# A chunked RWKV scan on one core: planned lengths, no fill matmuls, one direction with its halves swapped, and outputs stored by ScalarE's queue

## The chip, the cores and the metric

The kernel runs on one core of one Trainium2 chip. A core has five engines that run their own instruction streams in order and meet at semaphores: TensorE (PE; its weight loads are shown apart as PEld), VectorE (DVE), ScalarE (ACT), GpSimd (POOL) and SyncE (SP), which issues most of the transfers. The metric is the device time of one execution in microseconds; lower is better. Before the change it is 3036.94 us, the median of three runs (3034.74 to 3039.24).

## The reference

Two layers of a generator work on 1024 latent tokens and 256 context tokens of width 1024, in float32. The first layer mixes tokens with a bidirectional RWKV-7 scan, the second with a grouped 2-D Fourier transform; an MLP of hidden width 4096 follows each. The part that the change touches is the scan, which is run for 16 heads of width 64 in both directions:

```python
def step(s, inp):
    w_t, k_t, v_t, a_t, b_t = inp[:5]
    sa = jnp.einsum('bhvk,bhk->bhv', s, a_t)
    s = s * w_t[:, :, None, :] + sa[..., None] * b_t[:, :, None, :] + v_t[..., None] * k_t[:, :, None, :]
    y = jnp.einsum('bhvk,bhk->bhv', s, inp[5]) if with_out else None
    return s, y

for d in range(N_DIRS):
    rev = d == 1
    yc, s_ctx = _wkv_scan(st_c.get('r'), vh_c, *st_c['dirs'][d], s0, rev)
    yl, _ = _wkv_scan(st_l['r'], vh_l, *st_l['dirs'][d], s_ctx, rev)
```

The context gives the first 256 positions of each direction (no output is read from them), and the latents start from the state that it leaves.

## The kernel before, in words

**Stages.** The kernel projects the streams (up to about 634 us of the span), scans (634 to about 1250 us), and then does the readout, the two MLPs and the Fourier layer.

**Projections.** `factor` (L781) makes, for one direction and 128 channels, the four scaled factors of the scan in chunks of 64 positions, in the tiles `bk_` and `ar`, and stores them in DRAM (`s_bk`, `s_ar`). Four element-wise products on DVE or POOL (recorded at L460) write them.

**The scan.** It runs in 20 steps of 64 positions, 4 for the context and 16 for the latents; a step does both directions d for all 16 heads. In `scan_step`: the *scores* (L951) multiply the b and k factors with the a and r factors; ACT (L960, L964) and DVE (L967, L972) evict them with masks. The scores of b with a are a strictly triangular 64x64 matrix M per head and direction, and the recurrence inside a chunk needs the inverse of (1 - M). `scan_invert` makes it: DVE inverts 16x16 blocks (L1074 to L1104), PE joins them to 32x32 blocks with the matmul groups *H* (L1141) and *T* (L1154), and the 32x32 block off the diagonal of the 64x64 inverse comes from two more groups, *V* (L1173) and *G* (L1184): V = M's block times one diagonal inverse, copied out of PSUM (L427, tile `vt`), G = V times the other diagonal inverse, copied into the inverse's tile `tt` (L427 again). *turn* (L1130) transposes the b and k factors. After that comes the part that goes from step to step: *x* (L1008), a copy, *u* (L1017, which reads `tt`), copies into `sv`, *s* (L1031, the new state), an addition (L1037) and a scaling (L993) on DVE, and two copies of the state into the next step's `sv`. For latents the outputs are *r* (L1047) and *y* (L1053) into one bank, a copy by ACT into the tile `y` (L1059), and a store of 64x1024 values to `s_y`.

In H and T the four groups of 32 partitions each have their own rows and columns of the PE array. In V and G before the change the forward and backward direction both keep the off-diagonal block in the same place: V reads partition groups 0 and 2 only and writes 1 and 3, and G the other way round. So each is 32 matmuls of 32x32 on two groups, and the copies are two of 32x512 each.

**Order and queues.** The whole program is a list of operations with planned lengths. `Plan.emit` (L165) simulates the engines with these lengths and writes each engine's instructions in the order in which the simulation starts them. It also models PE's clock, which it takes to be halved when PE's weighted activity (`load`) of the previous interval was low. Where an operation opens a fresh PSUM bank and PE is planned to be idle before it, it writes *fill* matmuls into that bank (L230 to L233; the fill itself is L1843, identity times identity, and its result is overwritten). On the chip nothing looks at planned times any more: each engine takes its instructions in the written order and waits where a semaphore is not there yet.

SP issues the scan's loads (L916: `s_bk`, `s_ar`, `s_v`), the stores to `s_y` (also L916), and loads of modulation weights (L892, 128x512 pieces of `k_mwt`), which DVE multiplies and sums in between (L893). A store waits at SP for ACT's copy L1059, and what stands behind it at SP waits too. The ring of `y` tiles has two places, that of `bk` four.

```python
if e == "pe" and blank:
    fills = max(0, int((start - since - self.SLACK) / self.FILL))
    for _ in range(fills):
        since = self.clock(since, self.FILL, 1.0)
    start = max(start, since)
```

Of the kernel before, what the change touches and what calls it, by code (L numbers as in the profile page):

```python
# [18 lines left out]
P = 128  # L19
# [3 lines left out]
CTX = 256  # L23
# [57 lines left out]
class Plan:  # L81
# [10 lines left out]
    def __init__(self, nc, banks, engines, hold=None):  # L92
        self.nc, self.engines, self.hold = nc, engines, hold or (lambda d: 0.7)
        self.psum = Store(banks)
        self.ops, self.last, self.seen, self.uses = [], {}, {}, {}
        self.step, self.rank = None, 0.0
        self.dear, self.weigh, self.follows = {}, {}, {}
# [11 lines left out]
    def add(self, eng, dur, fn, r=(), w=(), bank=None, after=(), load=1.0, lag=None, hold=None):  # L109
        bases = [k[0] if isinstance(k[0], tuple) else k for k in (*r, *w) if not isinstance(k, Slab)]  # L110
        gates = []
        for k in bases:
# [3 lines left out]
            if g is not None:  # L116
# [4 lines left out]
                  hold=hold, dear=self.dear, weigh=self.weigh)  # L121
# [43 lines left out]
    def emit(self):  # L165
# [26 lines left out]
        while done < len(ops):  # L192
# [86 lines left out]
    ("bk", (8, P), *_row(4, "X0", 0, 1024)), ("mab", (2, 16, 32), *_row(3, "X1", 0, 1024)), ("tr", (16, 32), ("X1", 3072)), ("vt", (16, 32), ("X1", 3584)),  # L279
# [51 lines left out]
class Kernel:  # L331
# [449 lines left out]
    def factor(self, kt, low, d, c, k, k_k, kk, kkk, rr):  # L781
# [57 lines left out]
    def scan(self):  # L839
# [10 lines left out]
        for j, tt in enumerate(R["tt"]):  # L850
            for g in (1, 3):
                plan.add("pool", 0.6, lambda tt=tt, g=g: nc.gpsimd.memset(tt[32 * g : 32 * g + 32, :, 0:32], 0.0), (), [(("tt", j), g)])
# [4 lines left out]
        for i in range(NCH):  # L857
            self.plan.step = i
            self.scan_step(i)
# [47 lines left out]
    def scan_step(self, i):  # L907
# [3 lines left out]
        RZ = [[slice(hh * 64 + 32 * z, hh * 64 + 32 * z + 32) for hh in range(2)] for z in range(2)]  # L911
# [24 lines left out]
        for d in range(2):  # L936
# [5 lines left out]
            for h4 in range(2):  # L942
# [11 lines left out]
                plan.add("pe", 0.95, mms, [kb, (kL, "a", 0), (kL, "a", 1)],  # L954
                         [*BB, *[k for hh in range(2) for k in ((kM, d, hh, h4, 0), (kM, d, hh, h4, 1), (kL, "k", hh, h4), (k2, hh, h4))]])
                for hh, B in enumerate(BB):
# [4 lines left out]
                        mab[RZ[0][hh], :, ys].rearrange("p w q t -> p q w t"),  # L961
                        B.tile[RZ[0][hh]].rearrange("p (q w t) -> p q w t", q=4, w=4)[:, :, 0:2], AF.Copy, scale=-0.5),
                        [B], [(kM, d, hh, h4, 0)], B)
                    plan.add("act", 0.28, lambda bv=bv, hh=hh, ys=ys, d=d: nc.scalar.activation(  # L964
                        mab[RZ[1][hh], 0, ys], bv()[RZ[1][hh], :, 32:C], AF.Copy, scale=-0.5),
# [32 lines left out]
        for d in range(2):  # L998
# [11 lines left out]
            self.at = plan.add("pe", 0.95, x_mm, lall + vall, [B], B, load=0.95)  # L1010
# [9 lines left out]
            plan.add("pe", 0.95, u_mm, [kx, *kT], [U], U, load=0.5)  # L1020
# [3 lines left out]
            if i < NCH - 1:  # L1024
# [10 lines left out]
                plan.add("pe", 1.1, s_mm, vall + [(kt_, 0), (kt_, 1)], [B, kt0], B, load=0.78)  # L1035
# [3 lines left out]
            if lat:  # L1039
# [10 lines left out]
                def y_mm(B=Y, l2=l2, sv=sv):  # L1050
# [5 lines left out]
                plan.add("pe", 0.95, r_mm, vall + [E["ks"], (kL, "a", 0), (kL, "a", 1)], [Y], Y, load=0.5)  # L1056
                plan.add("pe", 1.05, y_mm, vall + [(k2, hh, h4) for hh in range(2) for h4 in range(2)], [Y], Y, load=1.0)
                y, ky = slot("y")
                plan.add("act", 0.58, lambda B=Y, y=y: nc.scalar.copy(y, B.tile), [Y], [ky], Y)  # L1059
                dma(self.s_y[d, E["lo"] - CTX : E["lo"] - CTX + C].rearrange("t (h c) -> h t c", h=2), y, 256, [ky],  # L1060
                    [("sy", d, (E["lo"] - CTX) // C)])

    def scan_invert(self, mab, kM, S):
# [60 lines left out]
        def turned(d):  # L1124
# [7 lines left out]
            plan.add("pe", 0.85, turn, [S[d]["kb"]], [*TB[d]], load=0.5)  # L1132
# [10 lines left out]
        for w in range(2):  # L1143
            plan.add("pe", 0.7, lambda w=w: h_mm(w), [kxt, *ms], [(H, w)], load=0.15)
# [11 lines left out]
        for w in range(2):  # L1156
            plan.add("pe", 0.75, lambda w=w: t_mm(w), [khp, kxd], [(T, w)], load=0.3)
# [11 lines left out]

        def v_mm():  # L1170
            for y in range(16):
                for g in (0, 2):
                    nc.tensor.matmul(V.tile[Q[g + 1], y * 32 : y * 32 + 32], mab[Q[g], 1, y, :], tr[Q[g], y, :], start=True, stop=True)  # L1173

        plan.add("pe", 0.75, v_mm, [ktr, *offs], [V], V, load=0.15)
        vt, kvt = slot("vt")
        for g in (1, 3):
            plan.flex({"act": 0.58, "dve": 0.69}, lambda e, g=g: self.copy_on(e, vt[Q[g]].rearrange("p y t -> p (y t)"), V.tile[Q[g]]),
                      [V], [(kvt, g)], V)

        def g_mm():
            for y in range(16):
                for g in (1, 3):
                    nc.tensor.matmul(G.tile[Q[g - 1], y * 32 : y * 32 + 32], vt[Q[g], y, :], tt[Q[g], y, 32:64], start=True, stop=True)  # L1184

        plan.add("pe", 0.75, g_mm, [(kvt, 1), (kvt, 3), (kT, 1), (kT, 3)], [G], G, load=0.15)
# [3 lines left out]
        return tt, [(kT, g) for g in range(4)] + [(kT, g, "o") for g in (0, 2)]  # L1190
# [40 lines left out]
    def late(self):  # L1231
        plan = self.plan
        plan.dear, plan.weigh = REST_DEAR, REST_WEIGH
# [635 lines left out]
def host_consts():  # L1869
# [8 lines left out]
    for hh in range(2):  # L1878
        b, k = slice(hh * 64, hh * 64 + 64), slice((1 - hh) * 64, (1 - hh) * 64 + 64)
        mask[b, 0, hh], mask[k, 0, hh] = np.concatenate([-0.5 * strict, -0.5 * incl], 1), np.concatenate([strict, incl], 1)  # L1880
        mask[b, 1, hh] = np.concatenate([-0.5 * strict, -0.5 * incl[:, ::-1]], 1)
        mask[k, 1, hh] = np.concatenate([strict[::-1], incl[::-1, ::-1]], 1)
# [72 lines left out]
```

## Time and profile before

| | |
|---|---|
| median of three runs | 3036.94 us (3034.74 to 3039.24) |
| the profiled execution: its own time, its span | 3052.24 us, 3050.2 us |
| mean granted TensorE clock of that execution | 0.947 of full speed |
| PE busy in the span | 2858.6 us (94%) |
| DVE, ACT, POOL busy in the span | 1880.4, 1014.3, 487.8 us |
| the scan stage, 634 to 1250 us | 616 us, PE busy 510.5 us, DVE 422.4, ACT 349.2 |

All times inside the execution are microseconds from the start of the span. A group of instructions is told as: line, engine, operation, output tile <- input tiles, shapes, count | busy us, mean ns of one | idle time of the engine ahead of them and what ended it. A float32 matmul appears as two matmul instructions in the trace, so 32 matmuls of the program are a group of x64.

### The profile page before, as it was taken

How to read it: one execution, taken by the hardware profiler on the slowest of the kernel's cores; microseconds unless marked ns; L12 is line 12 of the kernel's file. 1: busy time of each engine (PE TensorE's matmuls, PEld its weight loads, DVE VectorE, ACT ScalarE, POOL GpSimd, SP SyncE). 2: the span in 40 equal slices, each digit the busy share in tenths (PEclk: the TensorE clock that was granted, in tenths of full speed). 3: DMA queues.
4: the chain of work that ended last, by engine and by line, in shares of the span. 5: the costliest groups of instructions: out<-in, count | busy, mean ns of one | idle time of the engine just before them, and what ended most of it. 6: DMA issues, size and time to landing. Idle time of an engine off the chain costs nothing.

```text
span 3050.2 us, 63412 instructions
## 1 busy us (share of the span) xinstructions
PE 2858.6 (94%) x26844; PEld 2225.1 (73%) x26844; DVE 1880.4 (62%) x3363; ACT 1014.3 (33%) x1974; POOL 487.8 (16%) x415
## 2 busy tenths in 40 slices
PE   9999989988887888799999999999899999999998
PEld 5443446467777777688788888887798788888887
DVE  5398695546667666787655665454876554454455
ACT  4263454345555555333212111112322111111121
POOL 2063453300000000111110111010421110111110
PEclk9999999968789897799999999999899999999999
DMA  9266475623345443643222322211121111111111
GB/s 280 83 180 185 129 195 172 181 83 101 113 125 154 124 124 120 205 132 97 90 86 90 111 90 90 63 62 34 47 76 42 56 49 49 42 56 49 35 45 56
DMA packets 297293, 312.90 MB, mean 103 GB/s; under 512 B 81025, under 2 KB 212225, under 8 KB 297009
## 3 DMA queue, kind: packets, MB, share of 16 engines
q1 hardware_dynamic: 295648, 304.01, 33.3%
q8 instruction: 210, 3.44, 0.5%
q0 software_dynamic: 1360, 4.84, 0.5%
q14 instruction: 75, 0.61, 0.1%
HBM read 246.38 MB, written 62.39 MB: 101 GB/s over the span
## 4 chain that ended last, share of the span: by engine, by line
PE 78%; DVE 10%; DMA 4%; issue 4%; ACT 3%; SPq 1%; POOL 1%; DVEq 0%; ACTq 0%; POOLq 0%
PE ps L368 17%; PE ps L370 17%; PE ps L369 17%; PE ps L624 6%; PE ps L621 4%; PE ps L951 3%; PE ps L1843 2%; DVE bU L460 1%; PE ps L1008 1%; PE ps L1031 1%; PE ps L1017 1%; PE ps L1154 1%; PE ps L578 1%; PE ps L1053 1%; PE ps L1141 1%
## 5 line engine op out<-in xcount | busy, mean ns | idle before, releaser
L368 PE MATMUL ps<-rU,rU 128*128 128x512 f32 (+3 forms) x2632 | 980.1, 372 | 16.8 <-DVE rX L1538 8.0
L370 PE MATMUL ps<-rU,rU 128*128 128x512 f32 (+3 forms) x2632 | 976.1, 371 | 6.2 <-DVE rU L1268 3.5
L369 PE MATMUL ps<-rU,rU 128*128 128x512 f32 (+3 forms) x2632 | 975.9, 371 | 0.1
L368 PEld LDWEIGHTS ps<-rU,rU 128*128 128x128 f32 x2632 | 501.5, 191 | 111.9 <-DVE rX L1538 8.9
L370 PEld LDWEIGHTS ps<-rU,rU 128*128 128x128 f32 x2632 | 501.5, 191 | 97.8 <-DVE rU L1268 4.8
L369 PEld LDWEIGHTS ps<-rU,rU 128*128 128x128 f32 x2632 | 501.9, 191 | 90.3 <-DVE rU L1352 0.4
L1538 DVE SCALAR_TENSOR_TENSOR rX<-ps,mods,rX 128x512 f32<-128x512 f32 (+1 forms) x528 | 375.6, 729 | 123.8 <-PE ps L370 121.7
L1517 ACT ACTIVATE rS<-ps 128x512 f32<-128x512 f32 x122 | 73.0, 598 | 681.5 <-PE ps L370 680.8
L1268 POOL TENSOR_TENSOR rU<-rW,rU 128x512 fp32r<-128x512 f32 x73 | 118.0, 1621 | 1001.6 <-PE ps L370 518.3
L624 PE MATMUL ps<-bU,bU 128*128 128x512 f32 (+1 forms) x544 | 235.1, 568 | 2.6 <-ACT bS L427 1.9
L427 ACT CAST rU<-rW 128x512 fp32r<-128x512 f32 x161 | 97.2, 617 | 349.0 <-PE ps L370 260.9
L1268 DVE TENSOR_TENSOR rU<-rW,rU 128x512 fp32r<-128x512 f32 x201 | 173.3, 881 | 25.4 <-ACT rU L427 25.3
L427 DVE CAST rU<-rS 128x512 fp32r<-128x512 f32 (+1 forms) x97 | 45.0, 469 | 232.8 <-ACT rS L1520 205.4
L427 DVE CAST rU<-rW 128x512 fp32r<-128x512 f32 x115 | 55.1, 491 | 212.6 <-PE ps L369 210.3
L624 PEld LDWEIGHTS ps<-bU,bU 128*128 128x128 f32 x544 | 99.5, 191 | 108.2 <-issue 96.3
L621 PE MATMUL ps<-bU,bU 128*128 128x512 f32 x304 | 140.9, 604 | 0.0
L951 PE MATMUL ps<-sU,sX 64*128 64x128 f32 (+1 forms) x1280 | 119.3, 338 | 17.5 <-DVE sU L967 5.9
L951 PEld LDWEIGHTS ps<-sU,sX 64*128 64x128 f32 x1280 | 105.7, 241 | 24.7 <-issue 6.6
L427 ACT COPY sU<-ps 32x512 f32<-32x512 f32 (+1 forms) x167 | 96.2, 577 | 79.6 <-PE ps L1154 27.6
L967 DVE TENSOR_TENSOR sU<-ps,sW 64x256 f32<-64x256 f32 x160 | 67.5, 422 | 70.7 <-ACT sX L960 39.1
L1268 POOL TENSOR_TENSOR rU<-rS,rU 128x512 fp32r<-128x512 f32 x41 | 64.1, 1566 | 289.8 <-ACT rU L427 154.8
L1843 PE MATMUL ps<-ident 128*128 128x128 f32 x664 | 98.9, 308 | 2.8 <-DMA ident<-in_k_ident_dram 2.6
(275 smaller groups left out, 3740.8 us busy)
## 6 DMA issues: line engine op xcount, KB each, us to landing
rW<-in_mlp_w_dram SPq DMA_DIRECT2D x256, 256.0 KB
rW<-in_k_mwt_dram SPq DMA_DIRECT2D x96, 256.0 KB
sX<-s_bk SPq DMA_DIRECT2D x40, 512.0 KB
s_ar<-bU SPq DMA_DIRECT2D x32, 512.0 KB
sU<-s_ar SPq DMA_DIRECT2D x64, 256.0 KB
sW<-in_k_mwt_dram SPq DMA_DIRECT2D x64, 256.0 KB
bU<-in_rk_wk_dram SPq DMA_DIRECT2D x48, 256.0 KB
bU<-in_rk_wv_dram SPq DMA_DIRECT2D x48, 256.0 KB
```

Source lines behind the costliest of these rows:

```text
L368: nc.tensor.matmul(out, w[0], x[0], start=start, stop=False)
L369: nc.tensor.matmul(out, w[0], x[1], start=False, stop=False)
L370: nc.tensor.matmul(out, w[1], x[0], start=False, stop=stop)
L427: self.nc.scalar.copy(out, src) if e == "act" else self.engines[e].tensor_copy(out, src)
L621: fn = lambda B=B, x=x, w=w, ms=ms, kt=kt: nc.tensor.matmul(B.tile, x[:, ms], w, start=kt == 0, stop=kt == KT - 1)
L624: fn = lambda B=B, x=x, w=w, ms=ms, kt=kt, n=n: nc.tensor.matmul(B.tile[:, :n], w[:, ms], x[:, :n], start=kt == 0, stop=kt == KT - 1)
L951: nc.tensor.matmul(BB[hh].tile[:, j * P : j * P + nr], bk[HR[hh], q, :], L[hh][HR[hh], q, :nr], start=True, stop=True)
L967: plan.add("dve", 0.41, lambda bv=bv, ro=ro, hh=hh, q4=q4, d=d, L=L: nc.vector.tensor_tensor(L[hh][ro, q4, 0:C], bv()[ro, :, 0:C], self.ma ...
L1268: plan.flex({"dve": n / 960 + 0.07, "pool": n / 440 + 0.08}, lambda e: self.engines[e].tensor_tensor(out(1), src(), f32(out(0)), ALU.subtr ...
L1517: plan.flex({"act": 0.53, "dve": 0.6}, lambda e, B=B, s=s: nc.scalar.activation(s.tile[:, :512], B.tile, AF.Relu) if e == "act" else nc.ve ...
L1538: plan.add("dve", n / 960 + 0.12, lambda B=B, m=m, n=n, xs=xs: nc.vector.scalar_tensor_tensor(xs(), B.tile[:, :n], self.mod(layer, 5, m), ...
L1843: self.plan.fill = lambda t: nc.tensor.matmul(t[:, :P], self.ident, self.ident, start=True, stop=True)
```

## The change

Four things are done, all in the scan and in what feeds it.

1. *Halves swapped in direction 1.* For the backward direction the two halves of 32 positions of the a and b factors change places (in `factor`, in the score evictions and in the masks). The off-diagonal block then lies in partition groups 1 and 3 for the backward direction and in 0 and 2 for the forward one. V and G stay 32 matmuls each, but go over all four groups in turn, and each result takes 256 columns of 128 partitions in place of 512 columns of 64. V's two copies of 32x512 become one of 128x256; G's two copies of 32x512 become four of 32x256.
2. *Planned lengths.* The PE lengths that the plan uses are changed: scores 0.95 to 1.15, x and u 0.95 to 1.1, s 1.1 to 1.2, r 0.95 and y 1.05 to 1.15, H 0.7 and T 0.75 to 0.85 per half, turn 0.85 to 0.75, V and G 0.75 to 0.65.
3. *No fills* in the scan's steps from the fifth on (`bare`).
4. *The stores to `s_y`* are issued by ACT, planned at 0.1 us with the result 4.0 us later, and no longer by SP.

```diff
@@ Plan.emit
             if e == "pe" and blank:
-                fills = max(0, int((start - since - self.SLACK) / self.FILL))
+                fills = 0 if op["bare"] else max(0, int((start - since - self.SLACK) / self.FILL))
@@ factor
-        self.flex_tt(n, bk[:, :ng, 0], gv(ta), p1[:, :ng], ALU.mult, [kta, kp1], [(kbk, 0)])
+        hv = lambda ap: ap.rearrange("p g (w t) -> p g w t", w=2)
+        self.flex_tt(n, hv(bk[:, :ng, 0])[:, :, flip], hv(gv(ta)), hv(p1[:, :ng]), ALU.mult, [kta, kp1], [(kbk, 0)])
-        self.flex_tt(n, ar[:, :ng, 0], gr(kk), p0[:, :ng, 0:C], ALU.mult, [kkk, kp0], [(kar, 0)])
+        self.flex_tt(n, hv(ar[:, :ng, 0])[:, :, flip], hv(gr(kk)), hv(p0[:, :ng, 0:C]), ALU.mult, [kkk, kp0], [(kar, 0)])
@@ scan
             self.plan.step = i
+            self.plan.bare = i >= 4
             self.scan_step(i)
@@ scan_step
-                plan.add("pe", 0.95, mms, [kb, (kL, "a", 0), (kL, "a", 1)],
+                plan.add("pe", 1.15, mms, [kb, (kL, "a", 0), (kL, "a", 1)],
...
-            plan.add("pe", 0.95, u_mm, [kx, *kT], [U], U, load=0.5)
+            plan.add("pe", 1.1, u_mm, [kx, *kT], [U], U, load=0.5)
...
-                dma(self.s_y[d, E["lo"] - CTX : E["lo"] - CTX + C].rearrange("t (h c) -> h t c", h=2), y, 256, [ky],
-                    [("sy", d, (E["lo"] - CTX) // C)])
+                dst = self.s_y[d, E["lo"] - CTX : E["lo"] - CTX + C].rearrange("t (h c) -> h t c", h=2)
+                plan.add("act", 0.1, lambda dst=dst, y=y: nc.scalar.dma_start(dst, y), [ky], [("sy", d, (E["lo"] - CTX) // C)], lag=4.0)
@@ scan_invert
+        four = [(d, 2 * hh + d, 2 * hh + 1 - d) for hh in range(2) for d in range(2)]
+        own = lambda g: slice(32 * (g % 2), 32 * (g % 2) + 32)
         def v_mm():
-            for y in range(16):
-                for g in (0, 2):
-                    nc.tensor.matmul(V.tile[Q[g + 1], y * 32 : y * 32 + 32], mab[Q[g], 1, y, :], tr[Q[g], y, :], start=True, stop=True)
-        plan.add("pe", 0.75, v_mm, [ktr, *offs], [V], V, load=0.15)
+            for q in range(8):
+                for d, f, l in four:
+                    nc.tensor.matmul(V.tile[Q[l], q * 32 : q * 32 + 32], mab[Q[f], 1, 8 * d + q, :], tr[Q[f], 8 * d + q, :], start=True, stop=True)
+        plan.add("pe", 0.65, v_mm, [ktr, *offs], [V], V, load=0.25)
         vt, kvt = slot("vt")
-        for g in (1, 3):
-            plan.flex({"act": 0.58, "dve": 0.69}, lambda e, g=g: self.copy_on(e, vt[Q[g]].rearrange("p y t -> p (y t)"), V.tile[Q[g]]),
-                      [V], [(kvt, g)], V)
+        plan.flex({"act": 0.38, "dve": 0.42}, lambda e: self.copy_on(e, vt.rearrange("p q t -> p (q t)"), V.tile[:, :256]), [V], [kvt], V)
...
-        for g in (0, 2):
-            plan.flex({"act": 0.58, "dve": 0.69}, lambda e, g=g: self.copy_on(
-                e, tt[Q[g], :, 32:64], G.tile[Q[g]].rearrange("p (y t) -> p y t", y=16)), [G], [(kT, g, "o")], G)
+        for d, f, l in four:
+            plan.flex({"act": 0.38, "dve": 0.42}, lambda e, d=d, f=f, l=l: self.copy_on(
+                e, tt[Q[f], 8 * d : 8 * d + 8, own(l)], G.tile[Q[f], :256].rearrange("p (q t) -> p q t", q=8)), [G], [(kT, f, "o")], G)
```

The plan writes another order for the whole scan: of its 8154 PE matmuls (8062 after) 2955 stand in one common order, while PE's order ahead of the scan is the same and behind it 8551 of 8570 matmuls match. In the scan 115 fills become 7; the first run of 6 and a single one stay, in the first four steps. Three places show what moves.

PE around G and u in the thirteenth step (names: `ps` a PSUM bank, `sU`, `sS`, `sX` tiles of the scan; L1184 is G, L1017 u, L1008 x, L951 the scores). Before:

```order
L1008 MATMUL ps_95<-sU_188,sU_199 64x64
L1008 MATMUL ps_95<-sU_188,sU_198 64x64
L1184 MATMUL ps_94<-sU_173,sX_202 32x32 x32
L1843 MATMUL ps_96<-ident 128x128 x7
L1017 MATMUL ps_96<-sS_163,sU_173 64x64 x16
L951 MATMUL ps_91<-sU_191,sX_203 128x128
```

The same place after the change, where the lines are eight or six further on (L1192 is G, L1023 u, L1014 x, L957 the scores):

```order
L1014 MATMUL ps_95<-sU_188,sU_198 64x64
L1192 MATMUL ps_94<-sU_173,sX_202 32x32 x32
L1023 MATMUL ps_97<-sS_163,sU_173 64x64 x16
L1023 MATMUL ps_95<-sW_154,sU_173 64x64 x16
L957 MATMUL ps_91<-sU_191,sX_203 128x128
```

The seven fills between G and u are gone and nothing takes their place; both u groups now stand ahead of the next scores.

ACT around one copy of `y` after the change (L1065 is that copy, L1067 the store's issue; `sU_188<-sU_170` copies the state into the next `sv`, which x reads; `32x16x32` copies of `ps_94` are T's, the 128x256 one V's; L1140 evicts a turn):

```order
L1065 COPY sS_162<-ps_96 128x512
L1067 DMA s_y<-sS_162 2x64x512
L427 COPY sU_188<-sU_170 64x512
L427 COPY sU_172<-ps_94 32x16x32 x4
L1140 ACTIVATE sU_178<-ps_93,sS_160 128x512
L427 COPY sU_187<-sU_170 64x512
L427 COPY sW_154<-ps_96 128x512
L427 COPY sX_202<-ps_94 128x256
```

The store stands right behind its copy, as nearly everywhere, and ahead of a state copy and T's copies.

SP near the scan's end, where the last loads of `k_mwt` are issued (L892 before, L897 after; L1330 loads `k_xt` for the next stage). Before:

```order
L916 DMA s_y<-sS_161 2x64x512
L1330 DMA rX_12696<-in_k_xt_dram 128x4x256 x2
L916 DMA sU_189<-s_v 64x512 x2
L916 DMA s_y<-sS_162 2x64x512
L1330 DMA rX_12696<-in_k_xt_dram 128x4x256 x2
L916 DMA s_y<-sS_161 2x64x512
L892 DMA sW_159<-in_k_mwt_dram 128x512
L892 DMA sW_158<-in_k_mwt_dram 128x512
L892 DMA sW_157<-in_k_mwt_dram 128x512
```

And after:

```order
L922 DMA sU_189<-s_v 64x512 x2
L897 DMA sW_157<-in_k_mwt_dram 128x512
L897 DMA sW_156<-in_k_mwt_dram 128x512
L897 DMA sW_159<-in_k_mwt_dram 128x512
L897 DMA sW_158<-in_k_mwt_dram 128x512
L1264 DMA rW_12345<-s_y 128x2x256
L922 DMA sU_188<-s_v 64x512 x2
L897 DMA sW_157<-in_k_mwt_dram 128x512
```

The stores are gone from the queue, and all weight loads of the last steps stand ahead of the loads of `k_xt`.

More of the change, by code (lines that the diff above doesn't have):

```diff
@@ L1156, in scan_invert @@
         for w in range(2):
[L1157 removed]
+            plan.add("pe", 0.85, lambda w=w: t_mm(w), [khp, kxd], [(T, w)], load=0.3)
         turned(1)
@@ L1186, in scan_invert @@
[L1186 to L1190 removed]
+            for q in range(8):
+                for d, f, l in four:
+                    nc.tensor.matmul(G.tile[Q[f], q * 32 : q * 32 + 32], vt[Q[l], q, :], tt[Q[l], 8 * d + q, own(l)], start=True, stop=True)
```

44 lines of the change are left out of this document (23 added, 21 removed).

## The prediction

> **What bounds the kernel now.** I first read busy time by stage (columns: length, busy us of PE, its weight loads, DVE, ACT and POOL with counts, granted clock, share of the transfer engines, GB/s).
>
> ```profile
> 634.00:890.00 256.00, 219.78 (x6326) 203.35 (x6328) 180.48 (x422) 144.85 (x318) 5.17 (x10) 0.79 0.37 105
> 890.00:1250.00 360.00, 290.74 (x8974) 268.76 (x8974) 241.90 (x602) 204.30 (x427) 9.42 (x14) 0.85 0.44 133
> 1250.00:1700.00 450.00, 429.33 (x2794) 373.80 (x2795) 314.43 (x559) 119.21 (x211) 66.45 (x46) 0.96 0.36 114
> ```
>
> Behind 1250 us PE is busy 95% of the time at a clock of 0.96, and its order hardly changes there. In the scan, 616 us, PE is busy 510.5 us (83%) at a clock of 0.79 to 0.85, DVE 422 and ACT 349. So the scan is bound by PE's queue in its written order, with 105 us in which PE stands idle, and by a clock that is often halved. Next, the groups of that stage:
>
> ```profile
> L1173 PE MATMUL ps<-sX 32*32 32x32 f32 x1218 | 26.9, 204 | 19.2 <-ACT sU L427 14.2 <-DVE sU L427 5.0
> L1184 PE MATMUL ps<-sU,sX 32*32 32x32 f32 x1216 | 26.3, 201 | 9.3 <-ACT sX L427 4.5 <-DVE sX L427 3.6 <-issue 1.1
> L1154 PE MATMUL ps<-sU,sU 32*32 32x32 f32 x2560 | 35.8, 212 | 19.4 <-issue 19.4
> L1843 PE MATMUL ps<-ident 128*128 128x128 f32 x222 | 36.7, 320 | 0.0
> L960 ACT ACTIVATE sX<-ps 32x256 f32<-32x256 f32 x156 | 58.2, 373 | 77.8 <-PE ps L951 68.7 <-DVE sU L967 6.5
> L967 DVE TENSOR_TENSOR sU<-ps,sW 64x256 f32<-64x256 f32 x160 | 67.5, 422 | 70.7 <-ACT sX L960 39.1 <-DMA sW<-in_k_mask_dram 13.7 <-ACT sX L964 9.5
> L427 ACT COPY sX<-ps 32x512 f32<-32x512 f32 x32 | 18.5, 577 | 12.5 <-PE ps L1173 10.8 <-DVE sX L427 1.4
> ```
>
> V and G take 26.9 + 26.3 = 53.2 us, the fills 36.7. T, with twice the instructions of V, takes only 35.8, and its idle time is ended by nothing that the profile shows ("issue"): PE starves for instructions after dense runs of tiny matmuls. I take that part as unchanged.
>
> **V and G on four partition groups.** Single runs in order of time (start, length):
>
> ```profile
> 727.41 1.20 PE L1184 MATMUL ps<-sU,sX 32*32 32x32 f32 x64 [1.50 <-DVE sX L427]
> 1146.20 1.92 PE L1173 MATMUL ps<-sX 32*32 32x32 f32 x64 [1.43 <-DVE sU L427]
> 1009.37 0.73 PE L1141 MATMUL ps<-sU,sX 32*32 32x16 f32 x64
> 985.52 1.29 PE L1154 MATMUL ps<-sU,sU 32*32 32x32 f32 x128
> ```
>
> At full clock 64 instructions on two groups take 1.20 us (1.92 at the halved clock); on four groups H takes 0.73 for 64 and T 1.29 for 128. I take 0.70, so V and G lose 0.50/1.20 = 42% of 53.2, 22 us; times the 83% in which PE is busy at all, **-18 us**. At least -10, if half of it turns into waiting for the copies between V and G; at most -22.
>
> **The fills.** The order keeps 7 of 115, so 94% of 36.7 us, 34.5 us of PE work, goes. What counts is whether the next group was ready while PE filled. Four runs between G and u, with the copies of G that u needs:
>
> ```profile
> 906.28 3.78 PE L1843 MATMUL ps<-ident 128*128 128x128 f32 x16
> 907.00 0.69 DVE L427 COPY sU<-ps 32x512 f32<-32x512 f32 x1 [0.83 <-ACT sU L427]
> 909.99 2.08 PE L1017 MATMUL ps<-sW,sU 64*64 64x64 f32 x64
> ...
> 1031.57 1.83 PE L1843 MATMUL ps<-ident 128*128 128x128 f32 x14
> 1031.69 1.17 ACT L427 COPY sU<-ps 32x512 f32<-32x512 f32 x2
> 1033.33 0.86 PE L1017 MATMUL ps<-sS,sU 64*64 64x64 f32 x22
> ...
> 1094.25 1.60 PE L1843 MATMUL ps<-ident 128*128 128x128 f32 x12
> 1094.37 1.18 ACT L427 COPY sU<-ps 32x512 f32<-32x512 f32 x2 [1.19 <-PE ps L1184]
> 1095.78 2.08 PE L1017 MATMUL ps<-sW,sU 64*64 64x64 f32 x64
> ...
> 1188.30 2.27 PE L1843 MATMUL ps<-ident 128*128 128x128 f32 x18
> 1188.71 1.18 ACT L427 COPY sU<-ps 32x512 f32<-32x512 f32 x2
> 1190.51 1.15 PE L1017 MATMUL ps<-sW,sU 64*64 64x64 f32 x32
> ```
>
> From the copy's end to u's start: 2.30, 0.47, 0.23 and 0.62 us, together 3.62 of 9.48 us of fill. Some 0.2 of each is the hand-over (the shortest is 0.23), so 2.8 us, 30%, was lost; the rest covered a real wait, which stays as idle time. 30% of 34.5 is **-10 us**. The lower bound is nothing; the upper is the fills' share of the chain of waits through the stage:
>
> ```profile
> by line: PE ps L951 14.9%; issue 10.5%; PE ps L1008 6.5%; PE ps L1031 6.2%; PE ps L1017 5.1%; PE ps L1154 5.1%; PE ps L1053 4.6%; PE ps L1843 4.5%; PE ps L1141 4.3%; PE ps L1047 4.0%; DMA sW<-in_k_mwt_dram 3.7%; ACT sU L427 3.6%; PE ps L117
> ```
>
> 4.5% of 616 is 28 us.
>
> **The clock without fills** is the price on the other side. At the halved clock work takes 1.92/1.20, so a stretch loses 37% of its length. A fifth of the some 23 removed runs, followed by a halved stretch of 5 us (906.28 shows one that a fill did not prevent), cost 23/5 x 5 x 0.37 = **+8 us**. Nothing at best; the bad end is rival A.
>
> **The copies.** V's two copies of 577 ns become one of about 0.4 (L960 and L967 evict 256 columns in 373 and 422 ns), G's pair of 1.18 becomes four of 0.37 to 0.42 on two engines, some 0.8 to 1.0. That is up to 0.95 us in each of 20 steps, 19 us. But the new order puts an x group between V and G nearly everywhere, which covers V's copy in both versions; only G's copies, uncovered in the excerpt, count: 20 x 0.2 = **-4 us**.
>
> **The stores** leave SP for ACT.
>
> ```profile
> 1103.67 0.54 SPq L916 DMA_DIRECT2D s_y<-sS  x1
> 1231.35 3.94 SPq L916 DMA_DIRECT2D s_y<-sS  x1
> ...
> SPq L916 <- PE ps L1130: 81.3, 30, 14.6
> SPq L916 <- ACT sS L1059: 21.3, 9, 9.6
> ```
>
> An issue holds SP for 0.54 us, once for 3.94 behind a full queue. On ACT 32 x 0.54 = 17 us are added, and before each a wait for its own copy to be written, say 0.2 by the hand-over above: 24 us on an engine busy 57% of the stage. Queued behind are the state copies for x and T's copies, for which PE waits. A fifth on the path: **+5 us** (0 to +24). The trace shows no issue by ACT, so the price is SP's. By the Trainium skill, "DMA: Bandwidth & Descriptors", section on issuing engines not being separate queues, transfers of all issuers share the same engines and a second issuer saves only issue time; by that alone SP gains 17 us that it has to spare, and the next term would hold only what the order itself moves.
>
> **Loads that came late.** The chain has five long ones:
>
> ```profile
> 801.99 6.31 DMA sW<-in_k_mwt_dram
> 891.94 8.55 DMA sX<-s_bk
> 934.98 4.87 DMA sW<-in_k_mwt_dram
> 1056.69 6.45 DMA sX<-s_bk
> 1235.39 11.35 DMA sW<-in_k_mwt_dram
> ```
>
> 37.5 us. The `s_bk` loads could be issued only when a turn (L1130) gave its tile free (SP waited 81.3 us for turns); in the new order the turns mostly stand ahead of H, not behind T and V. SP no longer waits 21.3 us for `y`. The 11.35 us at the end stood behind `k_xt` loads and two stores; the order excerpt has these weight loads ahead. I take 14 of the 37.5: **-14 us**, with 0 and -37 as ends.
>
> **The rest.** Swapping halves changes only the order of elements in products whose views for the backward direction were already reversed; the same sizes, so 0 (it is hidden behind nothing, but adds no element). The longer planned lengths agree with rows such as 1.15 for L1017 x32, where 0.95 stood; the steps come out more regular. No row prices an order; of PE's 105 idle us I take a twentieth, **-5 us**, between -20 and +20.
>
> **Sum.** -18 - 10 + 8 - 4 + 5 - 14 - 5 = -38 us. The profiled execution took 3052.2 us, span 3050.2; it lies 0.5% above the median, which changes the sum by 0.2 us. 3036.9 - 38 gives **2999 us**.
>
> **Rivals.**
> A. *The clock falls.* Every step of the latents keeps its waits around H, T, V and G but no longer fills them, and PE stays halved into the score groups. Without the clock the terms give -46 us; a clock mean of 0.825 is 35% halved time, one of 0.67 is 66%. 31% of 570 us more, times 0.37, is +65: 3036.9 - 46 + 65 = 3056. It decides below a scan clock of about 0.72. For it: the halved V at 1146.20 behind a wait of 1.43 us, and the halved fills at 906.28. Against: the G at 727.41 runs at full clock behind a wait of 1.50, and V and G become denser. The Trainium skill, "TensorE: Matmul & The Clock Gate", section "Why this matters for your kernels", asks for no idle gaps beyond some 3 us; by it the removed runs, mostly under 2.3 us, would be harmless, and the clock's term would be 0.
> B. *ACT becomes the link.* A quarter of its issues are held like the 3.94 row: 8 x 3.4 = 27 us more, 3026.
> C. *It buys nothing.* PE's time in V, G and fills turns into waits for copies and instructions, so that the change does not do what it says; only the last load's part is left: 3034.
> D. *More.* All late loads and the fills' whole chain share go: -22 - 28 + 8 - 4 + 5 - 37 - 5 = -83, 2954.
>
> **How the numbers follow.** The forecast 0.67, A 0.10, B 0.08, C 0.08, D 0.07. The range 2964 to 3036 leaves out A, D and the edge of C. A measurement of this kernel tells 0.2%, 6 us, from no change. Faster: the forecast, D and most of B, 0.80. Same: most of C and a bit of B, 0.08. Slower: A and the rest, 0.12.
>
> **What would show it.** V and G at 0.7 us for x64 at full clock; 14 fill instructions in the scan in place of 222, with idle time of some 1 us between G and u; a scan clock of 0.78 or more (below 0.72 says A); ACT's issue at 0.54 us, with few waits of PE on ACT behind it; no `k_mwt` or `s_bk` load of over 6 us in the chain; and a scan that ends near 1212 us of the span with the stages behind it as long as now. If the gain came from behind the scan, or the scan's PE idle time grew by what V, G and the fills gave up, I would be wrong.

## The result, and the profile after

The change takes 3018.15 us (median of 8 runs, 3015.14 to 3023.4) against 3037.73 of the kernel before on the same chip (8 runs): a ratio of 0.9937, 95% interval 0.9919 to 0.9955, or 19.6 us less. I had forecast 2999 us, 38 us less. The direction was right, and about half of the size came.

The profile after, busy time by stage, the scan's two parts and the readout (columns as for the rows of before):

```profile
634.00:890.00 256.00, 203.53 (x6131) 187.30 (x6131) 186.58 (x456) 142.61 (x327) 7.02 (x13) 0.78 0.40 117
890.00:1220.00 330.00, 261.20 (x9089) 239.72 (x9087) 244.59 (x608) 190.69 (x418) 8.85 (x15) 0.88 0.47 139
1250.00:1700.00 450.00, 436.78 (x2521) 376.24 (x2520) 301.38 (x534) 112.34 (x196) 64.90 (x45) 0.98 0.33 103
```

The clock in the scan is 0.78 and 0.88 (before 0.79 and 0.85), though the fills are gone. The groups of that stage:

```profile
L1183 PE MATMUL ps<-sX 32*32 32x32 f32 x1280 | 16.7, 201 | 12.2 <-ACT sU L427 3.9 <-issue 2.9 <-DVE sU L427 2.8
L1192 PE MATMUL ps<-sU,sX 32*32 32x32 f32 x1280 | 17.4, 203 | 8.0 <-ACT sX L427 4.9 <-issue 3.2
L1160 PE MATMUL ps<-sU,sU 32*32 32x32 f32 x2560 | 35.3, 212 | 19.0 <-issue 18.2 <-DVE sU L1152 0.7
L1851 PE MATMUL ps<-ident 128*128 128x128 f32 x14 | 3.4, 419 | 0.0
```

V (L1183) and G (L1192) take 34.1 us in place of 53.2, the fills 3.4 in place of 36.7. T's idle time behind "issue" is as it was.

To see where the time went, I cut every trace of this study at the same two marks: the first and the last matmul of G. That window in the trace from which I predicted:

```profile
676.50:1254.80 578.30, 475.32 (x14754) 438.98 (x14754) 395.63 (x961) 325.07 (x685) 13.07 (x21) 0.85 0.42 125
```

In a second trace of the kernel before:

```profile
677.60:1247.20 569.60, 470.75 (x14752) 435.47 (x14754) 395.59 (x961) 324.81 (x685) 12.31 (x21) 0.86 0.42 127
```

And in the change:

```profile
680.10:1219.60 539.50, 427.46 (x14560) 392.35 (x14558) 401.59 (x988) 308.01 (x681) 13.59 (x25) 0.86 0.45 132
```

The scan shrank by 38.8 us against the first trace, by 30.1 against the second, whose whole execution (3042.85 us) is nearer to the median. PE's busy time fell by 43.3 us against the second, its idle time inside grew from 98.9 to 112.0. The scan's first G comes 2.5 us later, and from the last G to the end it takes 1798.3 us (span 3017.9) in place of 1793.7 (span 3040.9). So of 43 us of PE work saved, 13 became waits and 7 were given back around the scan.

The transfers of over 4.5 us in the chain of waits up to the scan's end, in the second trace of before:

```profile
933.51 5.04 DMA sW<-in_k_mwt_dram
1056.07 7.66 DMA sX<-s_bk
1227.80 11.39 DMA sW<-in_k_mwt_dram
```

And in the change, where the last two rows are already loads of the readout:

```profile
748.58 6.37 DMA sW<-in_c_dram
994.67 5.01 DMA sW<-in_c_dram
1092.96 8.77 DMA sX<-s_bk
1112.38 17.45 DMA s_y<-sS
1210.19 6.19 DMA rW<-s_y
1220.06 10.46 DMA rW<-in_rk_g_dram
```

No `k_mwt` load is left, but others stand in their place, an `s_bk` load among them, and a store of 17.45 us that was no part of the chain before.

### The profile page after: what moved, and what is told of

Same layout as the page of the kernel before. It is cut to its first block, busy times and chain, and to the rows that moved or that the text cites. A ratio compares the mean times of both kernels' runs of the same rounds, so it can differ in the third digit from the quotient of the medians.

```text
span 3017.9 us, 62948 instructions
## 1 busy us (share of the span) xinstructions
PE 2809.8 (93%) x26630; PEld 2176.4 (72%) x26630; DVE 1879.9 (62%) x3382; ACT 998.2 (33%) x1971; POOL 489.8 (16%) x423
## 4 chain that ended last, share of the span: by engine, by line
PE 69%; DVE 12%; issue 5%; ACT 3%; DMA 3%; POOL 0%; SPq 0%; ACTq 0%; DVEq 0%; POOLq 0%
PE ps L368 17%; PE ps L370 17%; PE ps L369 17%; PE ps L621 4%; PE ps L624 3%; PE ps L957 2%; PE ps L1037 1%; ACT sU L427 1%; DVE bU L460 1%; PE ps L1160 1%; DVE sU L973 1%; PE ps L1059 1%; DVE rU L1276 1%; PE ps L1147 1%; PE ps L1023 1%
## 5 line engine op out<-in xcount | busy, mean ns | idle before, releaser
L368 PE MATMUL ps<-rU,rU 128*128 128x512 f32 (+3 forms) x2632 | 980.1, 372 | 15.6 <-DVE rX L1546 8.0
L427 DVE CAST rU<-rS 128x512 fp32r<-128x512 f32 x96 | 44.6, 470 | 230.9 <-ACT rS L1528 203.6
L624 PEld LDWEIGHTS ps<-bU,bU 128*128 128x128 f32 x544 | 100.3, 193 | 109.3 <-issue 97.8
L957 PE MATMUL ps<-sU,sX 64*128 64x128 f32 (+1 forms) x1280 | 121.7, 338 | 18.2 <-DVE sU L978 6.3
L957 PEld LDWEIGHTS ps<-sU,sX 64*128 64x128 f32 x1280 | 107.6, 240 | 28.4 <-DVE sU L978 7.6
L427 ACT COPY sU<-ps 32x512 f32<-32x512 f32 (+2 forms) x186 | 95.9, 517 | 72.8 <-PE ps L1160 36.1
L621 PEld LDWEIGHTS ps<-bU,bU 128*128 128x128 f32 x304 | 56.5, 192 | 61.2 <-issue 57.8
```

Source lines behind the costliest of these rows:

```text
L368: nc.tensor.matmul(out, w[0], x[0], start=start, stop=False)
L427: self.nc.scalar.copy(out, src) if e == "act" else self.engines[e].tensor_copy(out, src)
L621: fn = lambda B=B, x=x, w=w, ms=ms, kt=kt: nc.tensor.matmul(B.tile, x[:, ms], w, start=kt == 0, stop=kt == KT - 1)
L624: fn = lambda B=B, x=x, w=w, ms=ms, kt=kt, n=n: nc.tensor.matmul(B.tile[:, :n], w[:, ms], x[:, :n], start=kt == 0, stop=kt == KT - 1)
L957: nc.tensor.matmul(BB[hh].tile[:, j * P : j * P + nr], bk[HR[hh], q, :], L[hh][HR[hh], q, :nr], start=True, stop=True)
```

## The experiments

All kernels are compared with the kernel before on the same chip. "Scan" is the time from the first to the last G in the one profiled execution, "behind" the time from there to the end; both, and PE's busy time, are of single traces.

| kernel | ratio to before, 95% interval | scan us | PE busy in it us | behind us |
|---|---|---|---|---|
| before, first trace | (3052.24 us) | 578.3 | 475.3 | 1795.4 |
| before, second trace | (3042.85 us) | 569.6 | 470.8 | 1793.7 |
| before, fills not issued | 1.0000 (0.9985 to 1.0014) | 568.8 | 457.9 | 1793.7 |
| before, `k_mwt` loads of one row | 0.9963 (0.9949 to 0.9977) | 556.2 | 459.3 | 1793.8 |
| halves and copies alone | 1.0022 (1.0009 to 1.0036) | 549.6 | 447.1 | 1821.7 |
| lengths alone | 1.0018 (1.0001 to 1.0035) | 577.9 | 455.4 | 1791.7 |
| **the change** | **0.9937 (0.9919 to 0.9955)** | 539.5 | 427.5 | 1798.3 |
| change, stores issued by SP | 0.9920 (0.9898 to 0.9942) | 534.5 | 424.3 | 1795.2 |
| change, stores issued by POOL | 0.9953 (0.9933 to 0.9973) | 552.3 | 434.0 | 1796.6 |
| change, stores planned for SP | 0.9922 (0.9902 to 0.9941) | 536.4 | 430.2 | 1794.6 |
| change, old lengths | 0.9992 (0.9977 to 1.0007) | 563.2 | 437.7 | 1797.4 |
| change, fills planned | 0.9985 (0.9968 to 1.0002) | 536.8 | 431.8 | 1820.2 |
| change, V and G twice | 1.0180 (1.0156 to 1.0204) | 627.5 | 469.4 | 1795.6 |
| change, half of H | 0.9851 (0.9832 to 0.9871) | 519.6 | 411.6 | 1797.0 |

**The kernel before, again.** No edit; a second trace.

> The kernel before, unchanged, for a second trace of it. Theory 1 (the forecast of -38 us was summed on an execution that was itself slow in the scan): the scan of this execution is 10 to 20 us shorter than in the first trace (first to last G 558 to 568 us there 578), the long loads of k_mwt at its end (11.35 us) and the two of s_bk (8.55 and 6.45 us) are mostly gone, and the whole time is 3030 to 3042 us. Rival (the excess of the first trace lay elsewhere, and the change's gain is given back outside the scan): first to last G is again 575 to 580 us, and the late loads are at the same places.

3042.85 us. Its chain has three late loads, 24.1 us, of which the trace that I predicted from had five, 37.5 us: the rows at 801.99 (6.31) and 891.94 (8.55) have no counterpart of over 4.5 us. So two of the five rows are not there in every execution of this kernel. The first of them is not peculiar to that trace either: the next kernel, which differs from this one only by its fills, has a `k_mwt` row of 6.01 us at 800.78 again.

**Fills not issued, order unchanged.**

```diff
-                for _ in range(op["fills"][0]):
+                for _ in range(0 if op["step"] is not None and op["step"] >= 4 else op["fills"][0]):
...
```

> The kernel before in its own order, only the 100 fill matmuls of the steps from the fifth on are not issued. Theory 1 (70% of a fill covers a wait that stays, and the clock falls a little): 0 to -10 us, with PE idle in the scan up by some 20 us. Rival A (the fills hold the clock): slower by 10 to 40 us, the scan's granted clock 0.05 or more lower. Rival B (the fills delay what was ready): -20 to -28 us.

The scan of this kernel:

```profile
677.00:1245.80 568.80, 457.89 (x14562) 425.20 (x14562) 394.11 (x960) 324.69 (x685) 12.62 (x21) 0.83 0.43 127
```

190 instructions fewer, and the clock falls from 0.86 to 0.83. In the second trace 210 fills take 35.5 us, so 190 are 32 us; PE's busy time fell only by 12.9, so the rest of its work took some 19 us longer, at the lower clock, and the idle time grew by 12. The total is nothing: of the 32 us, 19 came back as slower work and 12 as idle time.

**The change's order, with the stores issued by SP and by POOL in ACT's places, and stores planned for SP's queue anew.**

```diff
-... lambda dst=dst, y=y: nc.scalar.dma_start(dst, y), [ky], ...
+... lambda dst=dst, y=y: nc.sync.dma_start(dst, y), [ky], ...
```

With POOL it is `nc.gpsimd.dma_start`. The third plans them for SP:

```diff
-                plan.add("act", 0.1, lambda dst=dst, y=y: nc.scalar.dma_start(dst, y), [ky], [("sy", d, ...)], lag=4.0)
+                dma(self.s_y[...].rearrange("t (h c) -> h t c", h=2), y, 256, [ky], [("sy", d, ...)])
```

> The change in its own order on PE, ACT, DVE and POOL, but the stores to s_y issued by SP at the place that the plan gives them. Theory 1 (moving the stores to ACT's queue bought little, since a load and a store still wait for one another: each transfer from SP or ACT waits for the one eight before it): within 6 us of the change, 3012 to 3026 us, with SP now waiting for ACT's copy of y. Rival (the move was worth the 14 us of late loads that the forecast gave it): 10 to 20 us slower than the change, 3028 to 3038.

> The change in its own order, but the stores to s_y issued by POOL, whose transfers take no part in the eight marks that SP's and ACT's share. Theory 1 (in the change SP stood 67 us behind stores of ACT, and ACT once 6.4 us behind its own): SP's waits for s_y are gone and the time is 5 to 15 us below the change, 3003 to 3013. Rival (SP's loads come early enough, so these waits hide): within 5 us of the change, 3013 to 3023.

> The change with the stores planned for SP's queue as before (all else as in the change, planned anew; the run with the change's order and SP issuing took 3017 us). If the place of the stores is worth nothing: 3013 to 3027 us. If SP's queue, with the 32 issues and their waits back in it, makes loads late as in the kernel before: 3030 us or more, with late k_mwt or s_bk loads of over 6 us each, 14 us in all, back in the chain. If this order loses the passage to the readout as that of the halves alone did, the scan is near 540 us and the rest above 1815.

3017.36 and 3020.63 us with SP, against 3018.15 with ACT (0.9920 and 0.9922 against 0.9937): no difference that can be measured. With POOL it is 3026.32, 8 us more, with intervals that overlap, and outside both expectations, though SP waits for no store there; PE's idle time ended by "issue", summed over the rows of the waits between first and last G, rose from 62.8 to 78.7 us there. ACT's issue costs 0.50 us (median of 32), near the 0.54 of SP's row. What I had not seen is a new wait. SP's waits on the stores, in the change:

```profile
SPq L897 <- DMA s_y<-sS: 45.3, 9, 8.1
SPq L922 <- DMA s_y<-sS: 22.1, 4, 9.6
```

In the program as built, every transfer issued by SP or ACT signals one of eight completion counters, taken in turn, and waits until the transfer eight before it has landed (the trace's records name the counter of each transfer and the wait ahead of it). As long as SP issued everything, these waits were in its own order; with the stores on ACT the two queues wait for each other. SP's loads stood 67.4 us behind stores; with SP issuing, these rows are 0.3 and 4.7. Once ACT itself was held, by two stores in a row:

```profile
1129.91 0.50 ACTq L1067 DMA_DIRECT2D s_y<-sS  x1
1130.45 1.26 ACT L427 COPY sU<-sU 64x512 f32<-64x512 f32 x2 [6.41 <-DMA s_y<-sS]
```

This is the 17.45 us row of the chain above. With SP issuing, in the same order, the chain has no such row; the scan of that trace is 5.0 us shorter and the total is not told apart. So a long row in the chain is not its price. The Trainium skill, "DMA: Bandwidth & Descriptors", section on issuing engines not being separate queues, says that a second issuer saves only the time of issuing. The runs agree: the issues left SP, and 0.9937 is not told apart from 0.9920.

**Halves, V, G and their copies alone; lengths alone.** The first is the change with the fills, the stores and the lengths of x, u, s, r, y, H, T, scores and turn as before; the second the kernel before with only those lengths new.

```diff
-            self.plan.bare = i >= 4
+            self.plan.bare = False
...
-                plan.add("pe", 1.15, mms, [kb, (kL, "a", 0), (kL, "a", 1)],
+                plan.add("pe", 0.95, mms, [kb, (kL, "a", 0), (kL, "a", 1)],
...
-                plan.add("act", 0.1, lambda dst=dst, y=y: nc.scalar.dma_start(dst, y), [ky], [("sy", d, ...)], lag=4.0)
+                dma(self.s_y[...].rearrange("t (h c) -> h t c", h=2), y, 256, [ky], [("sy", d, ...)])
```

And on the kernel before:

```diff
-                plan.add("pe", 0.95, mms, [kb, (kL, "a", 0), (kL, "a", 1)],
+                plan.add("pe", 1.15, mms, [kb, (kL, "a", 0), (kL, "a", 1)],
...
```

> The swapped halves alone (V and G over four partition groups, one copy of V, four of G, with their planned lengths), on the other planned lengths of before, with fills and with SP's stores. Theory 1 (the forecast's terms for V, G and the copies, -18 and -4): 16 to 26 us faster than before. Rival (V and G are followed by waits in any case and PE's instructions arrive no faster; the gain of the whole change lies in the order): 0 to 8 us faster.

> The kernel before with the longer planned lengths of PE alone, with fills, SP's stores and the old V and G. Theory 1 (the order is worth little, the forecast had -5 for it): 0 to 8 us faster. Rival (the new order gives most of the gain, turns ahead of H and loads in time): 12 to 20 us faster.

The scan of the halves alone:

```profile
675.10:1224.70 549.60, 447.06 (x14734) 412.33 (x14732) 384.66 (x930) 314.91 (x691) 16.33 (x28) 0.86 0.42 124
```

Its chain at the passage from the scan to the readout, the long transfers:

```profile
1220.42 10.85 DMA rW<-s_v
...
1249.81 9.27 DMA rW<-s_y
1266.44 6.43 DMA sW<-in_k_mwt_dram
```

The scan is 20 us shorter, near what V, G and the copies should give (I had 18 + 4), but the plan wrote another order here too. All of it is lost at the passage, where the last scan steps and the readout's first loads now stand side by side: 28 us more behind the last G. The lengths alone leave the scan 8 us longer and the total 0.2% longer.

**The change with old lengths, and the change with its fills.** Each takes one part out of the change, and the plan writes the order anew.

```diff
-                plan.add("pe", 1.15, mms, [kb, (kL, "a", 0), (kL, "a", 1)],
+                plan.add("pe", 0.95, mms, [kb, (kL, "a", 0), (kL, "a", 1)],
...
```
```diff
-            self.plan.bare = i >= 4
+            self.plan.bare = False
```

> The change with the planned lengths of before (all else as in the change, planned anew). Halves alone shortened the scan by 20 us but lost 28 us at the passage to the readout. If the lengths are what keeps that passage whole, this kernel gains nothing: 3038 to 3046 us, the scan from first to last G near 545 us and 1815 us or more from there to the end. If it was the fills or the stores in SP's queue that spoilt the passage there, it is like the change: 3013 to 3023 us, and 1796 us behind the last G. If the lengths only slow the scan, it is faster than the change: below 3010.

> The change with its fills planned again in every step (all else as in the change, planned anew). Muted fills were worth 0 in the order of before. If they are worth 0 here too, the time is that of the change within what another order moves: 3013 to 3027 us, with a scan clock above 0.87. If the missing fills were worth 10 us as my term had them, or the order loses its passage as that of the halves alone did: 3028 us or more; the scan's length from first to last G (540 in the change) and what lies behind it (1798) tell which.

Both come out near the kernel before, by different ways. With old lengths the passage stays whole (1797.4), against my expectation, but the scan is 563.2, 24 us longer than in the change; 10 us of it is PE's busy time, 13 idle. With the fills planned the scan is as short as in the change (536.8, clock 0.88), but behind it 22 us are lost. Its long rows there:

```profile
1221.58 9.59 DMA s_y<-sS
1231.86 18.47 DMA s_y<-sS
1252.26 6.14 DMA sW<-in_k_mwt_dram
```

The two longest are stores of `y`, of which more below. So neither the lengths (+0.2% on the kernel before, planned anew) nor the missing fills (0 in the order of before) have a gain of their own, yet without either of them the change's gain is gone. What also differs is the order that the plan then writes. Why one order loses in the scan and another at the passage stays open.

**Late loads, priced by themselves.** The kernel before in its own order, with 60 of the 64 `k_mwt` loads carrying one row of 128; the sums made from them are then of older data.

```diff
-        self.plan.add("q", 0.8, lambda: nc.sync.dma_start(w(), src), (), [kw], after=after, hold=0.7)
+        self.plan.add("q", 0.8, lambda n=P if self.plan.step in (None, 3) else 1: nc.sync.dma_start(w()[:n], src[:n]), ...)
```

> The kernel before, in its own order, in which the scan's loads of k_mwt from the fifth step on carry one row of 128 (2 KB in place of 256 KB, 60 loads, 15.6 MB less); the modulation sums are then of older data. It prices the late loads by themselves: in the second trace of before the chain of waits holds two k_mwt loads of 5.04 and 11.39 us and one s_bk load of 7.66. If such a row is worth its length, as my term of -14 had it, the time falls by 16 us or more (by up to 24, if the s_bk load also comes earlier): ratio 0.992 to 0.995. If PE is held by its supply of instructions and a load that comes earlier only uncovers the next wait, it falls by 0 to 5 us: ratio 0.998 to 1.000, and other rows take the places in the chain.

11 us less (7 to 16 by the interval of the ratio), between the two expectations. But the long row that should have gone stayed. The chain's long transfers from 1000 us to the scan's end:

```profile
1049.46 8.22 DMA sX<-s_bk
1217.97 11.01 DMA sW<-in_k_mwt_dram
```

The last one carries 2 KB and still lands 11.01 us after its issue (11.39 with 256 KB). The transfer engines in the window from 1210 to 1235 us, in 40 slices, their mean busy share in tenths and what they moved:

```profile
DMA  6661117994993112111115721111111000391067
GB/s 200 203 203 64 49 46 193 374 334 134 305 360 128 61 52 79 48 49 48 49 48 177 267 75 52 52 49 52 49 49 46 3 3 0 87 326 36 0 152 267
```

From 1218 (the fourteenth slice) until the load lands, the share is a tenth or two and the rate some 50 GB/s, with a peak near 1224. What SP had issued ahead of the load, in its queue's order:

```profile
1204.85 1.30 SPq L1330 DMA_DIRECT2D rX<-in_k_xt_dram  x2
1207.25 3.00 SPq L916 DMA_DIRECT2D sU<-s_v  x2
1210.35 0.54 SPq L916 DMA_DIRECT2D s_y<-sS  x1
1210.94 4.28 SPq L1330 DMA_DIRECT2D rX<-in_k_xt_dram  x2
1215.32 2.55 SPq L916 DMA_DIRECT2D s_y<-sS  x1
1217.97 3.86 SPq L892 DMA_DIRECT2D sW<-in_k_mwt_dram  x3
```

That is 2.75 MB (512 KB, 128 KB and 256 KB each) within 13 us. The engines were not idle while the load waited: at 50 GB/s the two last stores of `y`, 512 KB, take 10.5 us, about the time of the load. A tenth or two as a mean over 16 engines is also what two of them give when they are always busy. In the change ACT's queue carries nothing but these stores; its row between the first and last G:

```profile
q10 hardware_dynamic: 3770, 7.60, 4.0%
```

4.0% of 16 times 539.5 us is 345 us of engine time for 30 stores, 11.5 us each. That a store runs on two engines, for 5 to 6 us when it has them to itself, is my estimate from these rows; the plan counts 4.0 us for it. A load that needs these engines would then wait for the stores, however small it is. This fits the Trainium skill, "DMA: Bandwidth & Descriptors", section "Queues, rings and completion order", by which a transfer's signal lands only behind all earlier writes of the same transfer engine. No run changed the form of the store.

What the kernel gained came from PE's busy time, 11.5 us less for the same instructions:

```profile
680.80:1237.00 556.20, 459.25 (x14752) 425.10 (x14754) 394.81 (x961) 325.01 (x685) 12.61 (x21) 0.87 0.35 103
```

A clock of 0.87 against 0.86 makes some 5 us of it; the rest stays open.

**More and fewer instructions on PE, in the change's order.** First V's and G's loop, then H's.

```diff
-            for q in range(8):
+            for q in [z for _ in range(2) for z in range(8)]:
...
-            for y in range(8 * w, 8 * w + 8):
+            for y in range(8 * w, 8 * w + 4):
```

> The change in its own order, with every matmul of V and G issued twice (same result): some 40 x 0.6 = 24 us more of PE work and 2560 more matmul instructions. Theory 1 (83% of V's and G's time lies on the path): 16 to 24 us slower than the change, 3034 to 3042. Rival 1 (waits for copies hide it): under 8 us slower. Rival 2 (PE is bound by how fast its instructions arrive): more than 24 us slower.

> The change in its own order with half of H's matmuls left out, so that half of the 32x32 inverses rest on what the bank held before; only the time is read. It takes 20 x 0.35 = 7 us of warm PE work and 2560 PE instructions (matmul and weight load) from the place just ahead of T. Theory (PE's idle time that nothing in the profile ends, 63 us in the scan, is the supply of instructions behind dense runs of small matmuls): that idle time falls by 10 us or more and the whole by 12 to 25 us. Rival (that idle time has another cause and only the work goes): 3 to 8 us faster than the change.

V and G issued twice: 75 us more than the change. Their groups, and T's, between first and last G:

```profile
L1192 PE MATMUL ps<-sU,sX 32*32 32x32 f32 x2558 | 32.4, 204 | 33.0 <-issue 30.5 <-ACT sX L427 2.5
L1160 PE MATMUL ps<-sU,sU 32*32 32x32 f32 x2432 | 32.4, 207 | 19.7 <-issue 19.3 <-DVE sU L1152 0.3
L1183 PE MATMUL ps<-sX 32*32 32x32 f32 x2432 | 28.6, 199 | 13.5 <-issue 7.6 <-ACT sU L427 3.0 <-DVE sU L427 2.8
```

In the change the same window has 17.4 and 15.6 us of G and V, with 3.2 and 2.9 us of "issue" ahead of them. So 28 us of work were added, and "issue" ahead of G grew from 3.2 to 30.5; over all of PE's groups it grew from 62.8 to 120.8. (The traced execution took 3110.11 us, 17 above the median of its kernel.) PE's busy time rose by 42 us, 14 more than the added work, at a clock of 0.83 in place of 0.86. Half of H left out, so that half of the 32x32 blocks hold older data, the other way; H, and T behind it:

```profile
L1147 PE MATMUL ps<-sU,sX 32*32 32x16 f32 x1216 | 15.7, 183 | 1.9 <-DVE sU L1123 1.5 <-issue 0.3
L1160 PE MATMUL ps<-sU,sU 32*32 32x32 f32 x2432 | 30.4, 202 | 34.2 <-issue 26.3 <-DVE sU L1152 7.9
```

H loses 13.2 us of work (28.9 before) and 11.1 us of "issue" ahead of it (11.4 before). Ahead of T "issue" grows from 18.2 to 26.3, but over all groups it falls from 62.8 to 47.1, and the kernel is 24 us faster.

What "issue" waits for, another row tells: the queue that the profile calls "instruction", between first and last G, in the change, with V and G twice, and with half of H:

```profile
q8 instruction: 113, 1.85, 1.4%
q8 instruction: 133, 2.18, 1.5%
q8 instruction: 104, 1.70, 1.4%
```

A packet has 16 KB, and there is one for some 257 matmuls and weight loads of PE (29118, 34108 and 26682 in the three windows). In the trace of the change all 39 "issue" waits of 0.5 us or more end 2.2 to 3.2 us after such a packet begins; points taken at random do so in 21% of cases. With V and G twice it is 61 of 64. So "issue" behind dense runs is the wait for PE's instructions, and it grows with their number: 2560 matmul instructions more cost 75 us, 1280 fewer gain 24, 1.8 to 2.7 times their own work.

## Why the prediction was right and wrong

- **V and G, and the copies (-18 and -4).** Right in PE's work. The groups lost 53.2 - 34.1 = 19.1 us; x64 in one run takes 0.75 us in 24 of 31 cases, where I had 0.70. The halves alone shorten the scan by 20, but with another order, and another order alone moved the scan by 8 and by 24 us. So that the 20 come from these terms is likely and not shown.
- **The fills and the clock (-10 and +8).** Near nothing in sum, as measured in the order of before, but by other shares: of 32 us of removed work, 12 stayed as idle time, where I had 70%, and the slower clock took 19, where I had 8. That the two errors cancel is luck. Rival A, the falling clock, did not come: 0.78 and 0.88.
- **The stores (+5).** Nothing can be measured: three kernels with SP or ACT issuing lie within 3.3 us. I priced ACT's issues rightly at 0.5 us, but queued only copies behind them; what was queued was SP, 67.4 us, through the shared counters. Nothing came of that either. Rival B fell.
- **Late loads (-14).** This step failed. I took the row's length as what goes when the load comes earlier. First, two of the five rows, 14.9 of 37.5 us, were not there in a second trace. Second, with 60 loads cut to 2 KB, the longest row stayed at 11.01 us, and the 11 us that this kernel gained came with PE's busy time, while PE's idle time hardly moved (98.9 and 97.0 us). Third, in the change no `k_mwt` row is left, but PE's idle time in the scan rose from 98.9 to 112.0: an `s_bk` row of 8.77 us is there still (SP waits 65.3 us for turns, 81.3 before), and the readout's loads and the stores of `y` stand in the chain now. My reason for the lateness of the last row named the `k_xt` loads and two stores ahead of it; by the rates above it was the stores, and the change keeps their form.
- **The order and the lengths (-5, between -20 and +20).** The mean was fair: from the halves alone to the change the scan lost another 10 us, and around it 7 were given back. Its ends were too near: the same edits with one part taken out move the scan by 24 us or the passage by 22.
- **"I take that part as unchanged"** (PE's hunger for instructions). In the change it nearly was: 56.7 us in the second trace of before, 62.8 after. But I used it nowhere. V and G keep their number of instructions, and ahead of them "issue" grew from 1.0 to 6.1 us, so part of what they saved went into waiting. Rival C, by which all of it would, did not come: of 43 us that PE saved, 13 became idle time.
- **"It lies 0.5% above the median, which changes the sum by 0.2 us."** This step failed too, and it made most of the miss. By their own working the terms are 48 us less PE work (22 and 34.5 less, 8 more) and 10 us more idle time (4, 24.5 and 5 more; 4, 14 and 5 less). Against the first trace, from which they were taken, the scan has 47.9 us less and 9.1 more, 38.8 us in all. So the sum fits that execution in its totals, with errors in the terms that cancel; but it was taken off the median, and that execution stood 14.5 us above it (the change's own traced execution 1.5 above its median). 8.7 us of this excess lie in the scan by the second trace, the stage from which I took every row. A sum made from a stage has to be taken off that execution's own stage, or off a second trace. Nearly all of the rest of the 18.4 us between forecast and result is the 6.5 us (against the first trace) that were given back around the scan, which I had taken as staying as long as it was.

Against the second trace the parts are: the kernel with the halves alone -20 in the scan, from there to the change another -10, which holds the order, the lengths and whatever late loads, fills and stores gave together, and +7 before and behind it: -23 between the two profiled spans, -19.6 between the medians. The runs don't part the -10 further.

## What to carry to other kernels

Take a second trace before pricing rare long rows, and price a late transfer by what stands ahead of it in its queue and what comes next when it is gone, not by its length in the chain. Take a sum off the execution whose rows it was made from. Where a planner writes the order anew, test an edit in the old order first: here three of five replannings moved the scan or the passage by 22 to 28 us, more than any single part of the change. In stretches of tiny matmuls count PE's instructions before its microseconds. A transfer can be slow on a few engines while the mean share of all looks idle: read the rate beside the share.

## What the runs showed of the hardware that was not expected

- PE's supply of instructions in dense runs of 32x32 matmuls: 2560 matmul instructions more cost 75 us for 28 us of work, 1280 fewer gave 24 us for 13.2. All 39 "issue" waits of 0.5 us or more in the change's scan end 2.2 to 3.2 us after a packet of the instruction queue begins.
- A 2 KB load, issued behind 2.75 MB in the same queue, landed 11.01 us later, while the transfer engines were a tenth or two busy and moved some 50 GB/s: by estimate two stores of 256 KB, each on two of 16 engines.
- SP waited 67.4 us on stores that ACT had issued, through completion counters that both queues use in turn, at no cost that could be measured.
- With 190 fills fewer in the same order the granted clock fell from 0.86 to 0.83, and the time stayed the same (1.0000, 0.9985 to 1.0014).
